# Gated DeltaNet stage of an encoder trunk: TensorE in program order, decays by one-hot products, a new tile order

## The chip, the core and the metric

The kernel runs on one core of a Trainium2 chip. The core has TensorE (PE; PEld is its weight load), VectorE (DVE), ScalarE (ACT), GpSimd (POOL) and SyncE (SP), which here issues every transfer. The metric is the time of one execution in microseconds (us) on the device, of which the median of several runs counts.

## What is computed

The reference is a trunk of two layers with four sub-layers: a mixer of pooling and sparse attention (e), a ConvFFN (f), a Gated DeltaNet mixer (o) and a second ConvFFN (f). Each sub-layer sits in the same frame, and the change concerns the third:

```python
def adaln_post_norm(x, c, mod_w, mod_b, ln_g, ln_b, sublayer):
    mod = jax.nn.silu(c) @ mod_w + mod_b
    shift, scale, gate = jnp.split(mod[:, None, :], 3, axis=-1)
    y = sublayer(x * (1.0 + scale) + shift)
    return layer_norm(DEEPNORM_ALPHA * x + gate * y, ln_g, ln_b)

def gdn_mixer(h, w_in, conv_w, a_log, dt_bias, out_norm, w_out):
    proj = h @ w_in                       # 512 x 1024 times 1024 x 4112
    qkv, gate, beta_raw, a_raw = jnp.split(proj, ODD_SPLITS, axis=-1)
    qkv = jax.nn.silu(causal_dwconv(qkv, conv_w))      # width 4
    ...                                   # 8 heads of 128; q, k normalised
    g = -jnp.exp(a_log) * jax.nn.softplus(a_raw + dt_bias)
    o = gated_delta_rule(l2_norm(q), l2_norm(k), v, beta, g)
    o = rms_norm(o, out_norm) * jax.nn.silu(gate)
    return o @ w_out
```

`gated_delta_rule` needs, for each head and block, decays exp(gc[i] - gc[j]) from the running sum gc of g, the matrix A of products of keys with these decays, the inverse of 1 + A, and then a recurrence over blocks of the sequence with a state of 128x128 for each head.

## The kernel before

**Precision.** A float32 operand is split into a part rounded to fp32r (`hi`) and the rest (`lo`), and a product is made of three passes, hi·hi, hi·lo and lo·hi (`mm3`, L97 to L102). For a weight tile ACT makes `wh` (L93), and DVE or POOL makes `wl` (L94).

**The projection** (`projs`, L144) multiplies the input, held transposed in `h`, with column tiles of 128 weights: 8 slices of the inner dimension, 3 passes, 24 products of 512 columns for each tile. There are 33 tiles: 16 columns for beta and a, then gates g0 to g3, keys k0 to k7, queries q0 to q7, values v0 to v7, gates g4 to g7. The first five are made in two halves of the sequence. Four PSUM buffers (`main`) take the results, three (`chain`) the other work, one (`side`) the modulation.

**Chains.** Each finished tile starts work that follows it: the convolution (`conv_silu`, one ACT pass L949, three DVE passes L951, a Silu L952), then a generator that goes one step further at each `pump` (L66). `k_chain` transposes k (L959), sums squares on ACT, forms A on DVE (L989) and stores it; `q_chain` likewise forms the attention products (L1009 to L1012); `v_chain` stores scaled values. `invert` (L1016) reads the 32x32 diagonal blocks of A back and solves them in 31 steps of two DVE operations (L1029, L1030). `y_chain` (L1040) joins the blocks of two heads into inverses of 128 with small products (L1057 to L1081). `decays` (L937) sends gc through DRAM (`gc_d`) to spread a row over 128 partitions, and makes exp(-|difference|).

**The side work** (`side`, L323) is no part of this sub-layer's data path. It multiplies x with the last norm's gain (`affine`), forms this sub-layer's gate (`mod_gate`, L302) and the shift and scale of the next (`mod_gb`, L286). For each of these three vectors `mod_acc` (L239) loads sixteen 256 KB pieces of a weight into the buffers `mr`, of which there are two; ACT multiplies a piece with c (L255), POOL adds it into `acc` (L257), of which there is one. The gate is spread over the partitions by two pairs of products with ones (L318, L319), whose operands lie in the same two `mr` buffers; shift and scale are summed by transposes (`sum_rows`, L283).

**The recurrence** (`step`, L1134 to L1177) goes over four blocks of 128. Its `state` (L1125) is a tile of the tag `acc`, so that its first write waits until the side work has let go of that buffer. The output projection and the second ConvFFN follow.

**The order.** Each engine executes in its own fixed order. A scheduler with a model of durations puts the instructions of all engines in order when the kernel is built; tile buffers are handed out in program order.

Of the kernel before, what the change touches and what calls it, by code (L numbers as in the profile page):

```python
# [14 lines left out]
P = 128  # L15
S = 512
# [10 lines left out]
class Trunk:  # L27
# [35 lines left out]
    def go(self, gen, rate=1):  # L63
        self.gens.append((gen, rate))
# [13 lines left out]
    BUFS = {"wr": 3, "wh": 5, "wl": 5, "h4": 8, "g4": 14, "t": 4, "c": 5, "sub": 1, "x": 4, "xn": 2, "gate": 1, "mr": 2, "acc": 1}  # L78
# [38 lines left out]
    EARLY = 4  # L117

    def tiles(self, kind):
# [3 lines left out]
        if kind == "o":  # L123
            cols = [(b + n * P, P) for b in (3 * D, D, 0, 2 * D) for n in range(8)]
            return [(4 * D, 16)] + cols[:self.EARLY] + cols[8:] + cols[self.EARLY:8]
# [18 lines left out]
    def projs(self, src, tiles, h, start=None, lo_eng=None):  # L144
# [5 lines left out]
        if start is None:  # L150
            ws = self.pre
            pss = [self.ps("main" if n < 4 else "side") for n in range(first)]
            for half in (slice(0, S // 2), slice(S // 2, S)):
                for n, (t, w, p) in enumerate(zip(tiles, ws, pss)):
                    inst = self.proj(p[:t[1]], w, h, half)
                    if half.start == 0 and n in self.TURN:
                        self.after(self.turns[self.TURN[n]], inst)
# [19 lines left out]
        AHEAD = 2  # L177
        ahead = [self.load_w(src, *t, lo_eng) for t in tiles[first:first + AHEAD]]
        for t, p in zip(tiles, pss):
            yield p[:t[1]]  # L180
        for n in range(first, len(tiles)):
            m = tiles[n][1]
            p = self.ps("main")
            self.proj(p[:m], ahead.pop(0), h)
            if n + AHEAD < len(tiles):
                ahead.append(self.load_w(src, *tiles[n + AHEAD], lo_eng))
            yield p[:m]
# [114 lines left out]
    def mod_gate(self, i):  # L302
# [9 lines left out]
        for h in range(2):  # L312
# [3 lines left out]
            nc.gpsimd.tensor_tensor(lo, part, hi.bitcast(F32), op=ALU.subtract)  # L316
            p = self.ps("side")
# [523 lines left out]
    def odd(self, i, l, h):  # L841
# [38 lines left out]
        gc_d = dram("gc_d", [NB, H, P])  # L880
# [5 lines left out]
        def gate(hd, p):  # L886
            gt = self.b("t", [P, S])
            self.silu = nc.scalar.activation(gt, p, AF.Silu)
            nc.sync.dma_start(og_d[hd], gt)

        def scalars(ba):
# [11 lines left out]
            self.after(inst, self.silu)  # L903
            self.after(nc.scalar.activation(alg, alg, AF.Exp), inst)
# [14 lines left out]
            mm(p[:32, NH:NH + P], g, up, start=True, stop=True)  # L919
            gr = self.b("c", [NH, P])  # L920
            nc.scalar.activation(gr, p[:32, NH:NH + P], AF.Copy)
            nc.sync.dma_start(gc_d.rearrange("t h s -> (t h) s"), gr)
            mm(p[:, :NH], up, g, start=True, stop=True)
            nc.vector.tensor_copy(gc, p[:, :NH])
# [4 lines left out]
            nc.scalar.activation(ex, p[:, :3 * NH], AF.Exp)  # L929
# [16 lines left out]
        def conv_silu(c0, p, out):  # L946
# [5 lines left out]
            inst = nc.scalar.activation(out, t, AF.Silu)  # L952
            self.after(inst, self.exp)
            return inst
# [19 lines left out]
        def k_chain(hd):  # L974
            yield
# [279 lines left out]
```

## Time and profile before

| | us |
|---|---|
| median of 3 runs | 1344.11 (1343.6 to 1347.73) |
| the profiled execution's own time | 1341.34 |
| its span, first to last instruction | 1339.6 |
| PE busy over the span | 1254.1 (94%) |
| DVE / ACT / POOL busy | 832.3 / 602.0 / 404.9 |
| mean granted TensorE clock | 0.971 |

Times within the profile count from the start of the span. A granted clock of 1.00 is the upper of TensorE's two levels (2.4 GHz); 0.50 would be the lower (1.2 GHz), and a stretch in between has had both. An engine's busy time counts each instruction once where they overlap. A row of waits names the engine that waited, the line it then ran, and what ended the wait.

### The profile page before, as it was taken

The numbers are of one execution on the slowest core, as the hardware profiler recorded it, in microseconds if no ns is written. First come the engines' busy times: TensorE is split into PE (matmuls) and PEld (weight loads), VectorE is DVE, ScalarE is ACT, GpSimd is POOL, SyncE is SP. The second block draws the span as 40 slices with busy tenths as digits, with TensorE's granted clock in tenths as the row PEclk, the third lists the DMA queues.
The fourth block names the chain that finished last, engine by engine and source line by source line (L and its number), as shares of the span: only waits on it lengthen the run. The fifth ranks groups of instructions, "written<-read, shape, count | busy, mean of one in ns | idle before, by whom it ended". The sixth has DMA issues, their size and how long they took to land.

```text
span 1339.6 us, 17376 instructions
## 1 busy us (share of the span) xinstructions
PE 1254.1 (94%) x6339; PEld 1023.6 (76%) x6339; DVE 832.3 (62%) x1374; ACT 602.0 (45%) x1107; POOL 404.9 (30%) x324
## 2 busy tenths in 40 slices
PE   4998999999999999999888878989899999999997
PEld 3666656888888888889676666878798888888885
DVE  5599853476877653463767994437647675555328
ACT  3565665653433342345366444545555343334220
POOL 4477666500100000017367675510281010000001
PEclk9999899999999999999988988989999999999998
DMA  9953444146555332513656438674144643323221
GB/s 271 241 166 106 155 149 136 35 127 214 186 180 172 127 110 95 143 48 98 156 165 175 125 102 204 197 261 145 59 127 126 204 128 100 103 79 110 95 63 63
DMA packets 227320, 185.79 MB, mean 139 GB/s; under 512 B 24813, under 2 KB 196058, under 8 KB 227234
## 3 DMA queue, kind: packets, MB, share of 16 engines
q1 hardware_dynamic: 227234, 184.68, 46.2%
q8 instruction: 50, 0.82, 0.3%
q14 instruction: 36, 0.29, 0.1%
HBM read 170.87 MB, written 13.65 MB: 138 GB/s over the span
## 4 chain that ended last, share of the span: by engine, by line
PE 66%; DVE 11%; DMA 10%; POOL 5%; ACT 4%; issue 3%; SPq 1%; DVEq 0%; ACTq 0%; POOLq 0%
PE main L99 16%; PE main L100 16%; PE main L101 16%; DMA mr<-in_f_mod_w_dram 3%; POOL acc L257 3%; PE chain L100 2%; PE chain L101 2%; PE chain L99 2%; DMA wr<-in_e_w_in_dram 2%; DVE t L951 2%; DVE xn L1030 2%; DVE sub L1029 2%; DMA mr<-in_o_mod_w_dram 1%; PE side L99 1%; PE side L100 1%
## 5 line engine op out<-in xcount | busy, mean ns | idle before, releaser
L100 PE MATMUL main<-h,wh 128*128 128x512 f32 (+3 forms) x1104 | 418.0, 380 | 1.7 <-DVE h L409 1.7
L99 PE MATMUL main<-h,wh 128*128 128x512 f32 (+3 forms) x1104 | 414.7, 381 | 2.3 <-ACT h L408 2.1
L101 PE MATMUL main<-h,wl 128*128 128x512 f32 (+3 forms) x1104 | 416.2, 378 | 0.0
L93 ACT ACTIVATE wh<-wr 128x1024 fp32r<-128x1024 f32 x176 | 184.2, 1049 | 292.3 <-PE main L100 196.7
L94 DVE TENSOR_TENSOR wl<-wr,wh 128x1024 fp32r<-128x1024 f32 x126 | 160.9, 1280 | 198.0 <-ACT wh L93 197.8
L99 PEld LDWEIGHTS main<-h,wh 128*128 128x128 f32 (+2 forms) x1104 | 208.9, 191 | 43.4 <-ACT h L408 3.1
L100 PEld LDWEIGHTS main<-h,wh 128*128 128x128 f32 (+2 forms) x1104 | 210.3, 191 | 40.2 <-DVE h L409 2.9
L101 PEld LDWEIGHTS main<-h,wl 128*128 128x128 f32 (+2 forms) x1104 | 210.0, 190 | 37.2 <-issue 0.4
L442 POOL TENSOR_TENSOR rstd<-rstd,mhalf 128x1 f32<-128x1 f32 x16 | 10.4, 650 | 523.2 <-DVE rstd L441 511.7
L94 POOL TENSOR_TENSOR wl<-wr,wh 128x1024 fp32r<-128x1024 f32 (+1 forms) x50 | 119.6, 2396 | 52.1 <-ACT wh L93 45.0
L257 POOL TENSOR_TENSOR acc<-acc,mr 128x512 f32<-128x512 f32 x84 | 109.2, 1306 | 68.4 <-ACT mr L255 60.9
L489 DVE SCALAR_TENSOR_TENSOR t<-main,cw,t 128x511 f32<-128x511 f32 (+1 forms) x164 | 121.5, 744 | 2.1
L255 ACT ACTIVATE mr<-mr,cs 128x512 f32<-128x512 f32 x84 | 60.2, 721 | 80.6 <-DMA mr<-in_f_mod_w_dram 49.8
L951 DVE SCALAR_TENSOR_TENSOR t<-main,ocw,t 128x511 f32<-128x511 f32 (+2 forms) x72 | 53.3, 741 | 32.4 <-ACT t L949 31.5
L487 ACT ACTIVATE t<-main,cb,cw 128x512 f32<-128x512 f32 x82 | 62.3, 761 | 0.0
L310 POOL TENSOR_TENSOR acc<-acc,mr 1x512 f32<-1x512 f32 x8 | 11.8, 1488 | 143.2 <-issue 71.5
L494 ACT ACTIVATE t<-t 128x512 f32<-128x512 f32 x42 | 26.4, 629 | 61.9 <-DVE t L489 61.6
L99 PE MATMUL main<-wh,h 128*128 128x512 f32 x128 | 50.2, 392 | 0.0
L100 PE MATMUL main<-wl,h 128*128 128x512 f32 x128 | 50.0, 391 | 0.0
L101 PE MATMUL main<-wh,h 128*128 128x512 f32 x128 | 49.8, 390 | 0.0
L356 DVE TENSOR_TENSOR h<-chain,h 128x256 fp32r<-128x256 f32 x48 | 19.5, 419 | 35.1 <-ACT h L355 34.7
L352 ACT ACTIVATE chain<-chain,B,G 128x128 f32<-128x128 f32 x84 | 33.1, 438 | 9.9 <-PE chain L344 9.6
(383 smaller groups left out, 2103.4 us busy)
## 6 DMA issues: line engine op xcount, KB each, us to landing
wr<-in_f_w_up_dram SPq DMA_DIRECT2D x84, 512.0 KB
wr<-in_f_w_down_dram SPq DMA_DIRECT2D x42, 512.0 KB
mr<-in_f_mod_w_dram SPq DMA_DIRECT2D x64, 256.0 KB
wr<-in_o_w_in_dram SPq DMA_DIRECT2D x32, 512.0 KB
g<-in_e_mod_w_dram SPq DMA_DIRECT2D x32, 256.0 KB
g<-in_f_mod_w_dram SPq DMA_DIRECT2D x16, 512.0 KB
g<-in_o_mod_w_dram SPq DMA_DIRECT2D x16, 512.0 KB
wr<-in_e_w_in_dram SPq DMA_DIRECT2D x11, 512.0 KB
```

What stands on the lines that cost most here:

```text
L93: nc.scalar.activation(hi, src, AF.Copy)
L94: (lo_eng or nc.vector).tensor_tensor(lo, src, hi.bitcast(F32), op=ALU.subtract)
L99: inst = mm(ps, l[0], r[0], start=start, stop=False)
L100: mm(ps, l[0], r[1], start=False, stop=False)
L101: mm(ps, l[1], r[0], start=False, stop=stop)
L255: inst = nc.scalar.activation(r, raw, AF.Copy, scale=c)
L257: nc.gpsimd.tensor_tensor(part, part, r, op=ALU.add)
L352: nc.scalar.activation(t[:, c, :], t[:, c, :], AF.Identity, scale=G[:, k:k + 1], bias=B[:, k:k + 1])
L487: nc.scalar.activation(t, p, AF.Identity, bias=cb[:, n:n + 1], scale=cw[:, 4 * NF + n:4 * NF + n + 1])
L489: nc.vector.scalar_tensor_tensor(t[:, k:], p[:, :S - k], cw[:, 2 * NF * (2 - k) + n:2 * NF * (2 - k) + n + 1], t[:, k:], op0=ALU.mult, op1 ...
L951: nc.vector.scalar_tensor_tensor(t[:, k:], p[:, :S - k], cw[:, 24 * (3 - k) + n:24 * (3 - k) + n + 1], t[:, k:], op0=ALU.mult, op1=ALU.add)
L1029: nc.vector.tensor_tensor(tv, As[:, j + 1:, j:j + 1].to_broadcast([P, n, m]), Xs[:, j:j + 1, :m].to_broadcast([P, n, m]), op=ALU.mult)
```

## The change

In the region of the projection PE now executes in program order (`manual_schedule`), and the other engines keep the scheduler. The chains are written later: `k_chain` and the others pass one or two pumps more before each product, so that PE meets them about two tiles after their tile. The order of tiles is a table (`ORDER`): g4 ahead of the keys, g5 among the queries. Four weight tiles get their `wl` on DVE instead of POOL (`QUIET`). The decays come from products with one-hot rows, without DRAM. The side work starts at k2 with one step a pump instead of three at q0, rests from q0 to g5, and goes on from q6 with one step a pump; what is left runs in `drain`, after the last tile. `t` has five buffers instead of four, and weights are loaded three tiles ahead instead of two.

```diff
-    BUFS = {..., "t": 4, "c": 5, "sub": 1, ...}
+    BUFS = {..., "t": 5, "c": 5, ...}
...
+    ORDER = [(t[0], int(t[1])) for t in ("g0 g1 g2 g3 g4 k0 k1 k2 k3 k4 k5 k6 k7 q0 q1 q2 q3 g5 "
+                                         "q4 q5 q6 q7 v0 v1 v2 v3 v4 v5 v6 v7 g6 g7").split()]
+    QUIET = [("q", 5), ("q", 6), ("q", 7), ("v", 0)]
+    YS = [("v", 1), ("v", 3), ("v", 5), ("v", 7)]
...
-            for half in (slice(0, S // 2), slice(S // 2, S)):
-                for n, (t, w, p) in enumerate(zip(tiles, ws, pss)):
-                    inst = self.proj(p[:t[1]], w, h, half)
+            for n, (t, w, p) in enumerate(zip(tiles, ws, pss)):
+                inst = self.proj(p[:t[1]], w, h, slice(0, S // 2))
...
-        AHEAD = 2
+        AHEAD = 3 if self.kind == "o" else 2
...
+        for t, w, p in zip(tiles, ws, pss):
+            if start is None:
+                self.proj(p[:t[1]], w, h, slice(S // 2, S))
             yield p[:t[1]]
...
         acc = yield from self.mod_acc(i, j)
+        yield
         o = self.s([P, KC], f"modc{j}")
...
             nc.gpsimd.tensor_tensor(lo, part, hi.bitcast(F32), op=ALU.subtract)
+            yield
             p = self.ps("side")
             nc.tensor.matmul(p, self.ones, hi, start=True, stop=False)
...
-        def decays():
-            for hd in range(H):
-                r = self.b("c", [P, NB, P])
-                nc.sync.dma_start(r, gc_d[:, hd:hd + 1, :].rearrange("t o s -> o t s").partition_broadcast(P))
-                nc.vector.tensor_tensor(r, r, bc(hcol(gc, hd), P), op=ALU.subtract)
-                nc.vector.scalar_tensor_tensor(r, r, -1.0, r, op0=ALU.mult, op1=ALU.min)
-                self.exp = nc.scalar.activation(dec(hd), r, AF.Exp)
+        def decays(heads):
+            for hd in heads:
+                p = self.ps()
+                for n, r in enumerate(self.rows):
+                    mm(p, sel[:, hd, :], r[0], start=n == 0, stop=n == 1)
+                nc.vector.tensor_tensor(v4(p), v4(p), bc(hcol(gc, hd), P), op=ALU.subtract)
+                nc.scalar.activation(p, p, AF.Abs)
+                inst = nc.scalar.activation(dec(hd), v4(p), AF.Exp, scale=-1.0)
...
         def k_chain(hd):
-            yield
+            for _ in range(3 if hd < 2 else 2):
+                yield
...
-            nc.vector.tensor_tensor(hcol(rb, hd), hcol(rk, hd), hcol(beta, hd), op=ALU.mult)
-            nc.vector.tensor_tensor(hcol(br2, hd), hcol(rb, hd), hcol(rk, hd), op=ALU.mult)
+            nc.gpsimd.tensor_tensor(hcol(rb, hd), hcol(rk, hd), hcol(beta, hd), op=ALU.mult)
+            nc.gpsimd.tensor_tensor(hcol(br2, hd), hcol(rb, hd), hcol(rk, hd), op=ALU.mult)
...
-        self.go(self.side(i), 3)
...
+        with self.tc.manual_schedule(engines={mybir.EngineType.PE}):
+            out = self.projs(win, self.tiles("o"), h, self.begin, lo)
...
+            for kind, hd in self.ORDER:
+                p = next(out)
...
+                elif kind == "k":
+                    conv(D + hd * P, p, kh(hd))
+                    if hd < 3:
+                        decays(range(3 * hd, min(H, 3 * hd + 3)))
...
+                    if hd == 2:
+                        side = self.go(self.side(i))
+                    self.go(k_chain(hd))
+                elif kind == "q":
...
+                    if hd in (0, 6):
+                        side[1] = hd // 6
+                    if hd == 2:
+                        self.go(invert())
...
+                if (kind, hd) in self.YS:
+                    self.go(y_chain(self.YS.index((kind, hd))))
+                self.pump()
         self.drain()
```

The order of instructions moves in three places that matter here. In the rows a number at the end of a name is a tile's own; L99 to L101 become L101 to L103, L318 and L319 become L330 and L331, L283 becomes L294, L252 becomes L262. The first place is PE where the gate's products (`side<-mr,ones`) stand. Before, the first pair is behind tile q5, and the second pair within q6 and q7:

```order
L100 MATMUL main_6372<-h_819_4162,wh_6200 128x512
L101 MATMUL main_6372<-h_815_4158,wl_6201 128x512
L318 MATMUL side_6428<-mr_6424,ones 128x512
L319 MATMUL side_6428<-mr_6425,ones 128x512
L99 MATMUL main_6494<-h_812_4155,wh_6300 128x512
```

Now both pairs stand behind g7, the last tile (`main_7287`):

```order
L102 MATMUL main_7287<-h_819_4162,wh_7066 128x512
L103 MATMUL main_7287<-h_815_4158,wl_7067 128x512
L330 MATMUL side_7315<-mr_7242,ones 128x512
L331 MATMUL side_7315<-mr_7243,ones 128x512
L1117 MATMUL chain_7323<-c_7265,c_7264 64x64 x8
L991 MATMUL chain_7333<-ident,t_7150 128x128 x4
L1100 MATMUL chain_7341<-c_7285,xn_6702 32x32 x16
L330 MATMUL side_7361<-mr_7319,ones 128x512
L1108 MATMUL chain_7372<-ident,g_1285_7201 64x64 x8
L331 MATMUL side_7361<-mr_7320,ones 128x512
```

The pairs moved by nine and more tiles to the end. The second place is SP, where the next sub-layer's shift and scale are loaded (`mr<-in_f_mod_w`). Before, the first of the 32 loads stands among the weights of the queries and values:

```order
L107 DMA wr_6931<-in_o_w_in_dram 128x8x128
L252 DMA mr_6441<-in_f_mod_w_dram 128x512
L884 DMA at_d<-c_6489 128x4x128
L252 DMA mr_6444<-in_f_mod_w_dram 128x512
L252 DMA mr_6447<-in_f_mod_w_dram 128x512
L107 DMA wr_7023<-in_o_w_in_dram 128x8x128
```

Now the first stands behind the last value that is stored, and the recurrence's loads (L1180) stand among them:

```order
L902 DMA og_d<-t_7312 128x512
L115 DMA wr_8029<-in_o_w_out_dram 128x1024
L895 DMA vb_d<-c_7338 128x4x128
L262 DMA mr_7366<-in_f_mod_w_dram 128x512
L1180 DMA xn_7564<-og_d 128x8x128
L262 DMA mr_7369<-in_f_mod_w_dram 128x512
L1180 DMA xn_7572<-og_d 128x8x128
L1180 DMA h_1359_7558<-vb_d 128x1024
L1180 DMA h_1360_7560<-kd_d 128x1024
```

All 32 loads moved behind the projection. The third place is PE between the first and the second block of the recurrence. Before, the last sums of the shift (`side<-ident,acc`) stand within the last tile, ahead of the recurrence's first product:

```order
L101 MATMUL main_7512<-h_814_4157,wl_7427 128x512
L1064 MATMUL chain_7443<-c_7397,xn_6812 32x32 x5
L283 MATMUL side_6958<-ident,acc_6715 128x128 x4
L1064 MATMUL chain_7443<-c_7397,xn_6812 32x32 x11
L99 MATMUL main_7512<-h_815_4158,wh_7426 128x512
```

Now all four sets stand behind the first block (L1207 to L1248), ahead of the second (L1195):

```order
L1222 MATMUL main_7606<-c_7586,h_1361_7562 128x128 x4
L1248 MATMUL chain_7682<-ident,h_1359_7558 128x128 x4
L1248 MATMUL chain_7690<-ident,h_1359_7558 128x128 x4
L294 MATMUL side_7461<-ident,acc_7365 128x128 x4
L294 MATMUL side_7467<-ident,acc_7365 128x128 x4
L294 MATMUL side_7538<-ident,acc_7474 128x128 x4
L294 MATMUL side_7544<-ident,acc_7474 128x128 x4
L1195 MATMUL main_7620<-acc_7557,g_974_5086 128x128 x2
```

The four sets moved from within the projection to between two blocks of the recurrence.

## Rows read from the trace of the kernel before

**Rows 1.** The page, part 1: busy time by engine.
```profile
PE 1254.1 (94%) x6339; PEld 1023.6 (76%) x6339; DVE 832.3 (62%) x1374; ACT 602.0 (45%) x1107; POOL 404.9 (30%) x324
```
**Rows 2.** Stretches: length, busy us of PE, PEld, DVE, ACT, POOL, clock, DMA share, GB/s.
```profile
626.50:892.00 265.50, 228.52 (x1244) 186.62 (x1244) 177.95 (x290) 128.47 (x289) 154.60 (x102) 0.92 0.62 173
735.00:805.00 70.00, 55.56 (x263) 45.56 (x261) 68.51 (x102) 29.15 (x86) 49.31 (x34) 0.93 0.45 118
880.00:900.00 20.00, 16.76 (x141) 13.88 (x141) 6.61 (x10) 8.14 (x14) 3.00 (x3) 0.83 0.82 303
```
**Rows 3.** Waits of PE from 626 to 892: total us, times, longest.
```profile
PE chain L959 <- ACT g L952: 13.0, 5, 4.3
...
PE side L283 <- POOL acc L257: 2.1, 2, 1.9
```
**Rows 4.** Timeline of PE: start, us; two products of a whole tile that follow each other.
```profile
650.12 0.39 PE L99 MATMUL main<-h,wh 128*128 128x512 f32 x1
650.35 0.39 PE L100 MATMUL main<-h,wh 128*128 128x512 f32 x1
```
**Rows 5.** Chain that ended last, 800 to 905: start, us to the next piece, what.
```profile
838.99 1.76 PE chain L1057 x16
...
845.04 1.02 PE chain L1064 x32
846.06 0.59 PE chain L959 x4
...
894.00 1.08 PE chain L1074 x16
...
895.75 1.14 PE chain L1081 x16
...
902.96 0.89 PE main L1152 x8
```
**Rows 6.** Timeline of DVE (then one row of POOL) around the inverse.
```profile
729.58 1.13 DVE L989 SCALAR_TENSOR_TENSOR g<-chain,br,g 128x128 f32<-128x128 f32 x4
...
741.18 0.20 DVE L1029 TENSOR_TENSOR sub<-xn,xn 128x31 f32<-128x31 f32 x1
...
754.03 2.44 DVE L1029 TENSOR_TENSOR sub<-xn,xn 128x192 f32<-128x192 f32 x1
...
757.87 0.37 DVE L1029 TENSOR_TENSOR sub<-xn,xn 128x207 f32<-128x207 f32 x1
...
803.93 1.03 DVE L1033 COPY xn<-xn 128x1024 f32<-128x1024 f32 x1
...
753.76 2.49 POOL L94 TENSOR_TENSOR wl<-wr,wh 128x1024 fp32r<-128x1024 f32 x1
```
**Rows 7.** Groups of DVE from 700 to 892: busy us, mean ns, idle before.
```profile
L1030 DVE TENSOR_TENSOR xn<-xn,sub 128x31 f32<-128x31 f32 (+15 forms) x31 | 23.3, 750 | 0.7
L1029 DVE TENSOR_TENSOR sub<-xn,xn 128x31 f32<-128x31 f32 (+15 forms) x31 | 22.6, 729 | 0.6
```
**Rows 8.** Line L1057, its products on PE: shortest, median, longest ns, first and last start.
```profile
L1057 PE MATMUL chain<-g,g x64: 217/275/294, 816.4 to 877.6; 128*128 128x64 f32 x64
```
**Rows 9.** Chain that ended last, 800 to 905, where it runs through the side work.
```profile
863.27 0.73 ACT mr L255
864.07 1.29 POOL acc L257
865.38 2.90 DMA mr<-in_f_mod_w_dram
868.37 0.73 ACT mr L255
869.17 1.30 POOL acc L257
870.49 2.83 DMA mr<-in_f_mod_w_dram
...
875.53 4.16 DMA mr<-in_f_mod_w_dram
```
**Rows 10.** Timelines of POOL and PE: last sum of the side work, first product of block 1.
```profile
883.97 1.27 POOL L257 TENSOR_TENSOR acc<-acc,mr 128x512 f32<-128x512 f32 x1 [2.14 <-ACT mr L255]
...
901.90 1.06 PE L1146 MATMUL main<-acc,g 128*128 128x128 f32 x8
```
**Rows 11.** Groups of POOL from 626 to 892: busy us, mean ns, idle before.
```profile
L316 POOL TENSOR_TENSOR mr<-acc,mr 128x512 fp32r<-128x512 f32 x2 | 2.8, 1387 | 0.0
```

More of the change, by code (lines that the diff above doesn't have):

```diff
@@ L63, in go @@
     def go(self, gen, rate=1):
-        self.gens.append((gen, rate))
+        item = [gen, rate]
+        self.gens.append(item)
+        return item
     def pump(self, n=1):
@@ L76, in drain @@
             self.pump()
-    BUFS = {"wr": 3, "wh": 5, "wl": 5, "h4": 8, "g4": 14, "t": 4, "c": 5, "sub": 1, "x": 4, "xn": 2, "gate": 1, "mr": 2, "acc": 1}
+    BUFS = {"wr": 3, "wh": 5, "wl": 5, "h4": 8, "g4": 14, "t": 5, "c": 5, "x": 4, "xn": 2, "gate": 1, "mr": 2, "acc": 1}
     def b(self, tag, shape, dt=F32):
@@ L176, in projs @@
                     next(start)
-        AHEAD = 2
-        ahead = [self.load_w(src, *t, lo_eng) for t in tiles[first:first + AHEAD]]
-        for t, p in zip(tiles, pss):
+        AHEAD = 3 if self.kind == "o" else 2
+        eng = lambda n: lo_eng[n] if isinstance(lo_eng, list) else lo_eng
+        ahead = [self.load_w(src, *t, eng(first + n)) for n, t in enumerate(tiles[first:first + AHEAD])]
+        for t, w, p in zip(tiles, ws, pss):
+            if start is None:
+                self.proj(p[:t[1]], w, h, slice(S // 2, S))
             yield p[:t[1]]
@@ L185, in projs @@
             if n + AHEAD < len(tiles):
-                ahead.append(self.load_w(src, *tiles[n + AHEAD], lo_eng))
+                ahead.append(self.load_w(src, *tiles[n + AHEAD], eng(n + AHEAD)))
             yield p[:m]
@@ L916, in scalars @@
             nc.vector.scalar_tensor_tensor(th(g), th(t3), -1.0, over(alg, NB), op0=ALU.mult, op1=ALU.mult)
+            yield
             p = self.ps()
[L919 to L924, printed above, removed]
+            for tb in range(NB):
+                mm(pc(p, tb)[:H], g[:, tb * H:(tb + 1) * H], up, start=True, stop=True)
+            for t in self.rows:
+                t.append(self.b("c", [H, S], F32R))
+            rh, rl = (t[0] for t in self.rows)
+            nc.scalar.activation(rh, p[:H], AF.Copy)
+            nc.vector.tensor_tensor(rl, p[:H], rh.bitcast(F32), op=ALU.subtract)
             p = self.ps()
@@ L951, in conv_silu, with silu @@
                 nc.vector.scalar_tensor_tensor(t[:, k:], p[:, :S - k], cw[:, 24 * (3 - k) + n:24 * (3 - k) + n + 1], t[:, k:], op0=ALU.mult, op1=ALU.add)
-            inst = nc.scalar.activation(out, t, AF.Silu)
-            self.after(inst, self.exp)
-            return inst
+            late.append(lambda: nc.scalar.activation(t if out is None else out, t, AF.Silu))
+            return t
+        def silu():
+            for fn in late:
+                inst = fn()
+                self.after(inst, self.exp)
+                if self.hold is None:
+                    self.hold = inst
+            late.clear()
         def tok_major(src):
@@ L1082, in y_chain @@
             nc.scalar.activation(y[:64, :, 64:], w64(p), AF.Copy)
-        YS = (1, 3, 5, 7)
-        out = self.projs(win, self.tiles("o"), h, self.begin, nc.gpsimd)
-        ba = self.b("c", [16, S])
-        nc.scalar.activation(ba, next(out), AF.Copy)
-        for hd in range(self.EARLY):
-            gate(hd, next(out))
-        scalars(ba)
-        decays()
-        for hd in range(H):
-            inst = conv_silu(D + hd * P, next(out), kh(hd))
-            if hd == 0:
-                self.hold = inst
-            self.go(k_chain(hd))
-            self.pump()
@@ L1117, in odd @@
-        for hd in range(self.EARLY, H):
-            gate(hd, next(out))
-            if hd + 5 in YS:
-                self.go(y_chain(YS.index(hd + 5)))
-            self.pump()
+        silus, late, self.exp, self.rows = [], [], None, ([], [])
+        sel = self.b("xn", [H, H, P], F32R)
+        nc.vector.tensor_copy(sel, self.ident[:H, :H].unsqueeze(2).to_broadcast([H, H, P]))
+        lo = [nc.gpsimd] * (len(self.ORDER) + 1)
+        for kind, n in self.QUIET:
+            lo[1 + self.ORDER.index((kind, n))] = nc.vector
```

83 lines of the change are left out of this document (51 added, 32 removed).

## The prediction

> **What bounds the kernel now.** I read four views: busy times, stretches, PE's waits, and the chain that ended last.
>
> PE is busy for 94% of the span [rows 1], so the end moves with what PE does and with where it stands still. The first five tiles of this stage end at 626.5 us and its last tile at about 892, and in these 265.5 us PE is busy for 228.5 at a mean clock of 0.92 [rows 2]. That is where the change can win. The waits there are single gaps of up to 4.3 us, most of them a key's or query's transposition that waits for the Silu [rows 3].
>
> A second bound hides beneath PE. From 816 to 881 the chain that ended last runs mostly through the side work: load a piece into `mr`, scale it on ACT, add it on POOL, and only then is its buffer free for the next load [rows 9]. The last of these sums ends at 885.2, the first product that reads the recurrence's state starts at 901.9 [rows 10], and PE waits for this work for 2.1 us in all [rows 3]. It is just in time now because it runs while PE still projects. The recurrence's state needs the `acc` buffer, so block 1 cannot start before the last of the three modulation vectors is summed.
>
> **The change, part by part.** I reckon two points: T, the end of the last tile (892 now), and S, the start of block 1 (901.9 now). Behind S the program is the same, so the time moves as S does.
>
> *PE's own work up to T.* At the upper clock a product of 512 columns follows the last after 0.228 us [rows 4]. 28 whole tiles of 24 come to 153.2. Sixteen key and query heads take four transposes (0.59) and eight product rows (0.89) each [rows 5], 23.7 together; eight values 4.7. A pair of heads in the joining of inverses costs 1.76 + 1.02 + 1.08 + 1.14, and about 0.54 for eight transposes at the rate of L1074 [rows 5], so four pairs 22.2. New are 16 one-hot products at 0.228, 3.7, and small ones for 1. Sum 208.5. By the order, 4.4 of it stands behind the last tile. T can't be earlier than 626.5 + 204.1 = 830.6.
>
> *The wait for the inverse.* PE can no longer go round a late operand, and the largest is the solved diagonal blocks that L1093 (L1057 before) reads behind tile v2. By the order, the last key's A stands behind tile q2: 626.5 + 12 tiles (65.6) + decays and small products (4.7) + eight transpositions (4.7) and eight sets of product rows (7.1) = 708.6. From A on DVE to the first step of the solution took 11.6, from 729.58 to 741.18 [rows 6], mostly A's way through memory, so 720.2. I add 5, because POOL and the DMA queue have two pieces of side work there for each tile. The solution then took 62.8, to 803.93 [rows 6], of which 45.9 were its own 62 operations [rows 7]; DVE was busy for 68.5 of those 70 us [rows 2]. From the copy at its end to L1057 passed another 12.5 [rows 6, 8].
>
> How long the 62 operations take depends on POOL. Of two nearly equal steps one took 2.44 us and one 0.37, and the long one lies on a POOL subtraction of 2.49 us [rows 6]. So I count 22 us for the operations alone and 8 for the short POOL operations that stay among them, as the order puts the weight subtractions of this stretch on DVE; with five tiles' convolutions, attention products and two subtractions (16) that is 46 instead of 62.8. The Trainium skill, SBUF — State Buffer, section Who interferes with whom, states that a VectorE instruction with two SBUF inputs is fully blocked by a GpSimd instruction that reads SBUF; the trace agrees, as the two rows show. By that rule alone, with POOL silent, the stretch would be 38 and T 8 us earlier; without it, at the old pace, T would be 17 later.
>
> So L1093 runs at 708.6 + 11.6 + 5 + 46 + 12.5 = 783.7. Behind it stand seven tiles (38.3), the joining but for its end (17.8) and five values (3.0), 59.1 in all: **T = 843**, between 831 (no wait) and 866 (inverse at its old pace and 6 more). Against 892 that is a gain of 49.
>
> *The side work behind T.* This is the price. The gate's two pairs of products now stand behind the last tile, and they read the two `mr` buffers. Until they have run, none of the 32 loads for the next shift and scale can start; before, they started among the queries and values. The second pair needs a copy on ACT and a subtraction on POOL of 1.39 us [rows 11] after the first: 5 us behind T, at 848. Then each buffer goes round through load (2.8 to 2.9 us, with a 4.2), ACT (0.73) and POOL (1.30), once in 5.1 us: from 865.38 to 870.49 and on to 875.53 [rows 9]. Two buffers make that 2.55 us a load, 81.6 for 32; the first two of each sixteen need no sum, which saves 2.6. The extremes are 2.43 (load, ACT and POOL with no gap) and 3.1 (with the load of 4.16). Among the first ten loads stand fifteen of 512 KB for the recurrence: 10.5 MB, 34.6 us at the highest rate of a stretch, 303 GB/s [rows 2], instead of 25.5, so 9 more (3 to 15). The turn between the two sums and the transposes and the state's copy at the end take 7. **S = 848 + 79 + 9 + 7 = 943**, 41 us later than now. Meanwhile PE has only block 0 of the recurrence.
>
> *Parts that cost nothing.* The decays lose their eight transfers through memory, which helps the keys begin earlier; that is in T, since no wait for Silus is left in it. Two ACT passes a head instead of one (8 × 0.6 us) lie on ACT, which is busy for 128 of 265.5 [rows 2]. The key factors on POOL and the third weight tile ahead lie beside PE; if POOL becomes the limit there, the 5 us above are too few. The other sub-layers get the same extra steps in their side work and nearly the same order; I count them as 0, within 2 either way.
>
> *Sum.* The profiled execution took 1341.3 and gains 41: 1382.3. It lies 2.8 under the median of the runs, so I forecast **1385**.
>
> **Rivals.** *The side work keeps up: faster.* If loads ran ahead and only POOL's 1.3 us counted, 32 pieces would take 41 us, and with T at 831 block 1 would start at 831 + 5 + 41 + 7 = 884, 18 earlier: 1326. It decides at 1.5 us a load for T = 843, or 1.8 for T = 831. For it speaks that all other traffic has then gone; against it that the load is the longest part of each round even at the end of the stage [rows 9], and two buffers can't hide it. The Trainium skill, Perfetto Trace Analysis, section Identifying the Most-Contended Engine, says to improve the engine with the highest occupancy first, which here is PE, and by that rule the filled gaps would come out as time saved; the trace agrees only up to T. Chance 0.08.
>
> *PE starves: much slower.* In program order each late operand stops all tiles behind it. If POOL (weights, sums and key factors in one queue) or the transfers fall behind, T comes at 866 or later, and with a slow round of the loads S lies at 975 to 995: 1417 to 1437. For it speaks how full DVE is around the inverse [rows 2]; against it that the chains stand two tiles behind and weights three tiles ahead. Chance 0.17.
>
> *The two cancel: no change.* With T = 831 and 1.8 us a load the time stays within 4 us. It needs both at once: 0.03.
>
> **How the numbers follow.** The forecast's own case, S later by 16 (T 831, 2.43 a load, 3 for the recurrence's loads) to 70, has 0.72, that is 1360 to 1414. A measurement of this kernel tells 0.3%, 4 us, from no change. Faster takes 0.08, the same 0.03, slower 0.72 + 0.17 = 0.89. The range leaves out the faster rival and the upper part of the starved case, and goes somewhat below the forecast's own lower end for an inverse and loads that both do better: 1352 to 1418.
>
> **What would show it.** Right: the last tile at 831 to 866; the gate's products directly behind it; 32 loads of `mr` behind them at about 2.5 us each; a gap of 70 to 90 us on PE before L1195, with the clock at its lower level in it, ended by POOL's sum and the transposes; block 1 at about 943, and from there on the old lengths. The inverse should lose its operations of over 2 us. Wrong: loads of that work between the tiles, a round of the buffers under 3.6 us, or block 1 before 902. If T lies beyond 870, the starved case holds.

## The result, and the profile after

The change takes 1407.56 us (median of 4 runs, 1402.83 to 1414.99) against 1345.92 for the kernel before in the same comparison: a ratio of 1.046, with a 95% interval of 1.040 to 1.052. The forecast was 1385 in a range of 1352 to 1418: the direction and the range hold, and the forecast is 23 us too low. The profiled execution took 1406.3, its span is 1404.6.

Page, part 1, busy time by engine; PE has the busy time of [rows 1] in a span 65 us longer:

```profile
PE 1254.5 (89%) x6359; PEld 1026.3 (73%) x6359; DVE 804.9 (57%) x1356; ACT 614.1 (44%) x1117; POOL 396.6 (28%) x336
```

Stretches of the changed kernel, columns as in [rows 2]; the first answers to its second row:

```profile
735.00:805.00 70.00, 56.63 (x273) 47.52 (x272) 55.57 (x103) 25.77 (x72) 34.91 (x22) 0.90 0.46 117
805.00:862.00 57.00, 57.00 (x438) 47.64 (x437) 23.03 (x33) 19.53 (x30) 8.85 (x7) 1.00 0.41 113
862.00:902.00 40.00, 16.73 (x156) 14.40 (x154) 11.54 (x15) 15.55 (x36) 9.20 (x7) 0.69 0.75 261
902.00:945.00 43.00, 2.23 (x8) 1.43 (x8) 2.06 (x6) 12.98 (x18) 19.31 (x16) 0.50 0.40 123
```

Around the inverse PE stands for 13.4 us, from 805 to 862 not at all; in the 83 us that follow it works for 19. What it waits for, 626 to 1000, answers to [rows 3]:

```profile
PE side L294 <- POOL acc L267: 63.1, 3, 34.6
PE chain L991 <- DVE c L1047: 8.9, 2, 6.2
PE chain L1248 <- DVE h L1241: 8.5, 1, 8.5
PE main L1207 <- DMA h<-vb_d: 6.9, 1, 6.9
PE chain L991 <- ACT g L976: 4.4, 1, 4.4
```

The wait for POOL's sum, 2.1 us before, is 63.1. Where the last tile ends, on PE's timeline:

```profile
862.40 0.40 PE L103 MATMUL main<-h,wl 128*128 128x512 f32 x1
862.63 0.39 PE L330 MATMUL side<-mr,ones 128*128 128x512 f32 x1
862.86 0.40 PE L331 MATMUL side<-mr,ones 128*128 128x512 f32 x1
...
865.87 0.50 PE L330 MATMUL side<-mr,ones 128*128 128x512 f32 x1
866.52 0.63 PE L1108 MATMUL chain<-ident,g 64*64 64x64 f32 x8
867.09 0.49 PE L331 MATMUL side<-mr,ones 128*128 128x512 f32 x1
```

The gate's products stand directly behind the last tile; the first load into a freed `mr` is issued at 866.4. The chain that ended last (start, us to the next piece) does not go through these loads at first. It runs through the last value's way through memory and block 0, and comes to a load of the side work only behind a load of the recurrence on SP's queue (SPq, L1180), which had waited for block 0:

```profile
865.67 5.69 DMA vb_d<-c
...
871.43 6.08 DMA h<-vb_d
...
877.55 3.48 PE main L1207 x16
...
898.20 0.37 SPq L1180
...
898.67 4.42 DMA mr<-in_f_mod_w_dram
```

From there it goes round like this until block 1 starts:

```profile
931.54 2.62 DMA mr<-in_f_mod_w_dram
934.24 0.73 ACT mr L265
935.03 1.27 POOL acc L267
936.32 2.62 DMA mr<-in_f_mod_w_dram
...
959.05 1.27 POOL acc L267
960.37 1.13 PE side L294 x4
...
964.82 2.08 PE main L1195 x8
```

A buffer's round is 4.78 us there (931.54 to 936.32), so 2.4 us a load with two buffers; 5.1 and 2.55 were reckoned from [rows 9]. The first product of block 1 is at 964.8, where it was at 901.9 [rows 10].

Three points hold the account. P is the 2100th product of the three-pass kind in the records, late in the sub-layer before this one (the expectations call it a triple product; a few records are missing, so it is good to about 1 us). T is the end of the last tile, S the first product of block 1.

| | P | T - P | S - T | end - S |
|---|---|---|---|---|
| before | 592.9 | 299.2 | 9.8 | 437.7 |
| change | 601.5 | 261.3 | 102.0 | 439.8 |
| difference | +8.6 | -37.9 | +92.2 | +2.1 |

The four sum to the 65.0 us by which the span grew. The stretch from P to T became 38 us shorter, and the tail behind it costs 92.

### The profile page after: what moved, and what is told of

It is laid out like the page before. It is cut to its first block, busy times and chain, and to the rows that moved or that the text cites. A ratio compares the mean times of both kernels' runs of the same rounds, so it can differ in the third digit from the quotient of the medians.

```text
span 1404.6 us, 17405 instructions
## 1 busy us (share of the span) xinstructions
PE 1254.5 (89%) x6359; PEld 1026.3 (73%) x6359; DVE 804.9 (57%) x1356; ACT 614.1 (44%) x1117; POOL 396.6 (28%) x336
## 4 chain that ended last, share of the span: by engine, by line
PE 69%; DVE 9%; DMA 8%; POOL 6%; ACT 4%; issue 2%; SPq 1%; DVEq 0%; ACTq 0%; POOLq 0%
PE main L101 17%; PE main L102 17%; PE main L103 17%; DMA mr<-in_f_mod_w_dram 3%; POOL acc L267 2%; PE chain L102 2%; PE chain L103 2%; PE chain L101 2%; POOL wl L96 2%; ACT mr L265 1%; PE side L101 1%; PE side L102 1%; PE side L103 1%; DVE xn L1066 1%; DMA mr<-in_o_mod_w_dram 1%
## 5 line engine op out<-in xcount | busy, mean ns | idle before, releaser
L101 PE MATMUL main<-h,wh 128*128 128x512 f32 (+2 forms) x1104 | 414.8, 380 | 2.4 <-ACT h L420 2.1
L102 PE MATMUL main<-h,wh 128*128 128x512 f32 (+2 forms) x1104 | 413.4, 375 | 1.9 <-DVE h L368 1.1
L103 PE MATMUL main<-h,wl 128*128 128x512 f32 (+2 forms) x1104 | 413.1, 375 | 0.0
L96 DVE TENSOR_TENSOR wl<-wr,wh 128x1024 fp32r<-128x1024 f32 x130 | 166.1, 1280 | 202.2 <-ACT wh L95 202.2
L101 PEld LDWEIGHTS main<-h,wh 128*128 128x128 f32 (+1 forms) x1104 | 207.9, 189 | 43.8 <-ACT h L420 2.7
L102 PEld LDWEIGHTS main<-h,wh 128*128 128x128 f32 (+1 forms) x1104 | 208.1, 189 | 40.3 <-DVE h L368 2.0
L103 PEld LDWEIGHTS main<-h,wl 128*128 128x128 f32 (+1 forms) x1104 | 208.2, 189 | 37.5 <-issue 0.4
L96 POOL TENSOR_TENSOR wl<-wr,wh 128x1024 fp32r<-128x1024 f32 (+1 forms) x46 | 109.7, 2388 | 59.8 <-ACT wh L95 46.6
L294 PE MATMUL side<-ident,acc 128*128 128x128 f32 x48 | 9.3, 326 | 64.3 <-POOL acc L267 63.1
L294 PEld LDWEIGHTS side<-ident,acc 128*128 128x128 f32 x48 | 6.7, 165 | 67.2 <-POOL acc L267 65.5
L506 ACT ACTIVATE t<-t 128x512 f32<-128x512 f32 x42 | 26.4, 629 | 59.1 <-DVE t L501 58.9
L101 PE MATMUL main<-wh,h 128*128 128x512 f32 x128 | 50.2, 392 | 0.0
L103 PE MATMUL main<-wh,h 128*128 128x512 f32 x128 | 49.8, 390 | 0.0
```

What stands on the lines that cost most here:

```text
L96: (lo_eng or nc.vector).tensor_tensor(lo, src, hi.bitcast(F32), op=ALU.subtract)
L101: inst = mm(ps, l[0], r[0], start=start, stop=False)
L102: mm(ps, l[0], r[1], start=False, stop=False)
L103: mm(ps, l[1], r[0], start=False, stop=stop)
L294: self.nc.tensor.transpose(p[:, k * P:(k + 1) * P], acc[:, k * P:(k + 1) * P], self.ident)
L506: nc.scalar.activation(av[0], av[0], AF.Silu)
```

## The experiments

Each ratio is to the kernel before, run on the same chip beside it. All the runs that have a time are in one table, P, T and S from one profile of each. e3, the changed kernel with four buffers `mr`, has none: its buffers need 200 KB a partition, and 196.75 KB are there.

| run | P | T | S | median us | ratio, 95% |
|---|---|---|---|---|---|
| e1, side work early | 598.4 | 880.7 | 901.1 | 1346.02 | 1.001 (0.999 to 1.003) |
| e2, before with it late | 599.4 | 871.3 | 972.5 | 1417.11 | 1.054 (1.050 to 1.058) |
| e4, steps only here | 596.3 | 856.2 | 959.5 | 1404.72 | 1.045 (1.040 to 1.050) |
| e5, three `mr` | 600.7 | 866.3 | 948.1 | 1388.52 | 1.032 (1.030 to 1.035) |
| e6, rest in the inverse | 600.5 | 896.8 | 916.9 | 1357.54 | 1.009 (1.007 to 1.012) |
| e7, and other subtractions | 602.4 | 896.8 | 918.0 | 1356.26 | 1.008 (1.005 to 1.010) |
| e8, before again | 595.1 | 894.8 | 904.6 | 1343.95 | one run |
| e9, free order on PE | 602.5 | 858.0 | 961.0 | 1401.82 | 1.041 (1.036 to 1.047) |
| e10, combined, three `mr` | 602.4 | 887.7 | 899.8 | 1337.12 | 0.994 (0.992 to 0.996) |
| e11, combined, two `mr` | 606.5 | 878.7 | 892.4 | 1335.59 | 0.990 (0.986 to 0.994) |
| e12, e11 with free order | 604.5 | 855.8 | 891.4 | 1331.74 | 0.987 (0.983 to 0.990) |
| e13, change again | 601.9 | 863.6 | 967.5 | 1409.73 | one run |

**e1: the side work early.** In the change the side work rests from q0 to q5, g5 among them; here it goes on.

```diff
-                        side = self.go(self.side(i))
+                        side = self.go(self.side(i), 2)
...
-                    if hd in (0, 6):
-                        side[1] = hd // 6
+                    if hd == 2:
+                        side[1] = 1
...
+                    side[1] = 2
                     v = conv(2 * D + hd * P, p)
```

> The changed kernel, with one thing undone: the side work goes at two steps a tile, one from q2 to q7, two again from v0, and never rests. So the gate's two pairs of products stand behind q3 and g5 on PE instead of behind the last tile, and the sums of scale and shift stand behind v2 and behind v7 and g6. Theory (the loss is the tail: from T = 862 to S = 965 PE waits for loads that could not start before the gate's products): loads start near 740, the last sum ends by 850, T stays at 862 to 880, block 1 starts 8 to 12 us behind T, at 872 to 890 instead of 965, and the time is 1313 to 1333, some 80 us under the change and 12 to 30 under the kernel before. Rival A (program order on PE is the loss, wherever the side work stands): the waits move between the tiles, T goes beyond 900 and the time stays over 1370. Rival B (POOL's sums now fall into the inverse and hold DVE): T 885 to 900, time about 1344, no gain over before.

Measured 1346.02. The tail is gone: S - T falls from 102 to 20, and S lies 64 us earlier than in the change. That is the theory's main claim, and it stands. But there is no gain over before, so the sum of the theory was wrong: T came at 881, and S 20 us behind it instead of 8 to 12. From its first step to the copy at its end the inverse took 55.5 us, where the change's took 46.7. PE's waits from 640 to 930:

```profile
PE chain L991 <- DVE c L1047: 10.5, 1, 10.5
PE chain L991 <- ACT g L976: 6.0, 1, 6.0
PE main L1208 <- DMA h<-vb_d: 4.1, 1, 4.1
PE side L294 <- DVE modc L295: 3.1, 1, 3.1
PE chain L1093 <- POOL acc L267: 2.9, 1, 2.9
PE side L331 <- POOL mr L327: 2.4, 1, 2.4
```

Rival A falls. Rival B's time fits, and its T nearly (881, where it had 885 to 900), but not all of its place: some waits lie around the inverse (the first two), others are PE's own turn at products and sums of the side work. How the 21 us by which T - P is longer than in the change divide between the two isn't shown. Behind T stand the joining's end (881 to 889), the wait for the last value's way through memory (4.1) and block 0 (893 to 901).

**e2: the kernel before, with the tail put in.** The scheduler, decays and tile order are those of before; the side work has the pace of the change, and its gate products are held behind the last tile's:

```diff
             p = self.ps("side")
-            nc.tensor.matmul(p, self.ones, hi, start=True, stop=False)
+            inst = nc.tensor.matmul(p, self.ones, hi, start=True, stop=False)
+            if self.kind == "o":
+                self.after(inst, self.last)
```

> The kernel before, scheduler, decays and tile order as they were, with one thing put in: the gate's products are held behind the last product of the last tile, as in the change, by the same slow and resting rate of the side work and an order on PE. Theory (the price is the tail): T stays at 885 to 892, the 32 loads start behind it and take 94 us as in the changed kernel, block 1 starts at 985 to 995 instead of 902, and the time is 1420 to 1440. Rival (manual order on PE, decays or tile order cost the time, not the place of the side work): the loads keep up behind T at POOL's pace of 1.3 us each, block 1 at 935 to 945, time 1375 to 1390, or no change at all at 1344.

Measured 1417.11, 3 us below the theory's 1420 to 1440 and far from either of the rival's times. The theory had T at 885 to 892 and block 1 at 985 to 995; they came at 871 and 972. PE's waits from 640 to 1000 begin with

```profile
PE side L286 <- POOL acc L260: 69.2, 3, 34.8
```

and S - T is 101.2, as in the change. So the place of two pairs of products, with the pace that puts them there, makes the whole loss without any of the other edits. The run shows a second thing that nobody had asked: T - P fell from 299.2 to 271.9. With the side work out of the way the old order gains 27 of the 38 us that the change gains. For the order of PE, the decays, the tile order and the other edits 10.6 are left. The stretch from P to T in the kernel before, in e2 and in the change, columns as in [rows 2]:

```profile
592.90:892.10 299.20, 262.22 (x1518) 218.58 (x1517) 189.83 (x319) 147.03 (x330) 176.11 (x112) 0.93 0.57 159
599.40:871.30 271.90, 244.89 (x1433) 205.16 (x1432) 175.69 (x307) 125.03 (x293) 139.30 (x83) 0.96 0.50 135
601.50:862.80 261.30, 245.17 (x1465) 206.71 (x1464) 155.44 (x287) 132.86 (x304) 133.57 (x95) 0.97 0.48 131
```

PE stands still for 37.0, 27.0 and 16.1 us of them. So 10 of e2's 27 us are shorter waits, and 17 are less busy time: fewer instructions stand ahead of T, and the granted clock is 0.96 instead of 0.93. The 10.6 that the other edits add are, in sum, waits alone. Which of those edits brings them isn't shown.

**e5: three buffers `mr`.**

```diff
-    BUFS = {"wr": 3, "wh": 5, "wl": 5, "h4": 8, "g4": 14, "t": 5, "c": 5, "x": 4, "xn": 2, "gate": 1, "mr": 2, "acc": 1}
+    BUFS = {"wr": 3, "wh": 5, "wl": 5, "h4": 8, "g4": 14, "t": 4, "c": 5, "x": 4, "xn": 2, "gate": 1, "mr": 3, "acc": 1}
```

> The changed kernel with three buffers mr instead of two, the place for it taken from t (four instead of five, as before the change). Theory (behind T two buffers going round through load, ACT and POOL in 4.84 us set 2.42 us a load): three make it 1.6 us, and POOL's 1.3 is not reached; the 24 loads of the second half take some 40 us instead of 57, the first ten gain less among the recurrence's loads, block 1 starts 17 to 28 us earlier, 937 to 948, and the time is 1380 to 1391. Rival (the transfers or the order on SP's queue set the pace): less than 6 us change, 1401 to 1412. Fewer t may hold up a tile here and there, 0 to 5 us, in T and not behind it.

Measured 1388.52, and S - T is 81.8 instead of 102.0: the theory's time, and a difference of its size. T - P is 265.6 instead of 261.3, within the 0 to 5 us allowed for the missing `t`. POOL's timeline in that run (start, us):

```profile
927.34 1.26 POOL L267 TENSOR_TENSOR acc<-acc,mr 128x512 f32<-128x512 f32 x1 [0.54 <-ACT mr L265]
929.28 1.26 POOL L267 TENSOR_TENSOR acc<-acc,mr 128x512 f32<-128x512 f32 x1 [0.68 <-ACT mr L265]
931.01 1.26 POOL L267 TENSOR_TENSOR acc<-acc,mr 128x512 f32<-128x512 f32 x1 [0.47 <-ACT mr L265]
```

A sum every 1.7 to 1.9 us instead of 2.4: the number of buffers sets the pace once the recurrence's loads are through, and the rival, under 6 us of change, falls. The theory's place for the gain holds only in half. From T to the issue of the seventeenth load passed 48.8 us instead of 58.8, and from there to S 33.0 instead of 43.2, so 10 of the 20 us came in the first sixteen loads, though the theory expected less gain among the recurrence's loads.

**e6 and e7: the side work around the inverse.** In e6 it takes two steps a tile up to q1, none until q6, then two from q7, so that its additions miss the inverse, and the sums of shift are held behind the last tile (those lines are left out below); e7 is e6 and moves the subtractions that DVE takes over:

```diff
...
+                if side is not None:
+                    side[1] = {"q2": 0, "q7": 2, "v4": 3, "v5": 2, "g6": 1}.get(f"{kind}{hd}", side[1])
...
-    QUIET = [("q", 5), ("q", 6), ("q", 7), ("v", 0)]
+    QUIET = [("v", 0), ("v", 1), ("v", 2), ("v", 3), ("v", 4)]
```

> The changed kernel with the side work laid around the inverse: two steps a tile from k2 to q1, none from q2 to q6, two from q7 (gate's products behind q7 and v0), both sums of scale behind v4, and the sums of shift held behind the last tile. In the run with the side work early POOL's 1.3 us additions fell into the inverse, DVE had ten steps of over 1 us there, and T was 881 instead of 862. Theory (the additions in the inverse cost those 18 us): the inverse is as in the changed kernel (737 to 786), T 860 to 868, loads from 790 to 872, block 1 at 880 to 892, time 1321 to 1334. Rival (T at 881 came from waits of PE for the side work's own products, which stand between the tiles again): T 875 to 885 and block 1 at 895 to 905, time 1338 to 1350.

> The kernel of the run before in this list, and the weight subtractions that DVE takes over from POOL are those of v0 to v4 instead of q5, q6, q7 and v0, since in the changed kernel those of v1 to v4 ran on POOL inside the inverse (747, 755, 765, 773), each beside a step of 2.4 us. Theory (a POOL operation holds a DVE step for its length): four steps of 2.4 us fall to 0.4, four subtractions of 1.2 come, the inverse ends 3 to 5 us earlier and the time falls by as much. Rival (DVE is the full engine there, 19.3 of 20 us, whoever holds it): no change within 2 us.

e6 missed: 1357.54, slower than both guesses. The inverse is as the theory had it (736.4 to 786.2), but T is 896.8, for a reason of its own. First row of PE's waits from 640 to 960 in e6:

```profile
PE side L296 <- POOL acc L269: 20.0, 1, 20.0
```

Behind the second pair of products, at 787.6, the sixteen loads of the scale took until 837.6, 3.1 us each beside the weights instead of the 2.5 that I had reckoned, and PE stood in front of the sums with five tiles behind them. So e6 can't tell its theory from its rival, and whether the additions in the inverse cost T 18 us stays open.

e7 can be read, since the inverse lies ahead of that wait. Two steps of it in the change, on DVE's timeline:

```profile
746.27 1.38 DVE L1065 TENSOR_TENSOR c<-xn,xn 128x231 f32<-128x231 f32 x1
747.68 2.45 DVE L1066 TENSOR_TENSOR xn<-xn,c 128x231 f32<-128x231 f32 x1
```

The weight subtraction on POOL's timeline that lies on the second:

```profile
747.34 2.53 POOL L96 TENSOR_TENSOR wl<-wr,wh 128x1024 fp32r<-128x1024 f32 x1
```

And the same two steps in e7 on DVE's timeline, with the subtraction now behind them there:

```profile
746.84 1.38 DVE L1069 TENSOR_TENSOR c<-xn,xn 128x231 f32<-128x231 f32 x1
748.25 0.40 DVE L1070 TENSOR_TENSOR xn<-xn,c 128x231 f32<-128x231 f32 x1
...
749.46 1.22 DVE L97 TENSOR_TENSOR wl<-wr,wh 128x1024 fp32r<-128x1024 f32 x1
```

The step of 2.45 is one of 0.40; all four steps over 2 us are gone, and the inverse's own operations take 26.3 us, where e6's took 33.5. Yet from its first step to the end of its copy it takes 48.5 instead of 49.8, and it ends 1.1 us earlier, not 3 to 5. DVE spends most of what the steps no longer lose on the work that it took over: weight subtractions take 6.1 us of that stretch instead of 1.2, and the copy takes 2.2 instead of 1.1. The rival's forecast holds, no change within 2 us, but the time is no test of the inverse here, as the 20 us wait lies behind it in both runs. The Trainium skill, SBUF — State Buffer, section Who interferes with whom, states that a VectorE instruction with two SBUF inputs contends with a GpSimd instruction that reads SBUF, and that the ports they share are an exclusive lock; the rows agree for the single step. The stretch shows that handing the blocking work to DVE gives back only the difference.

**e4, e8, e13: why P is late.** e4 keeps the two added steps of the side work in this sub-layer only:

```diff
         acc = yield from self.mod_acc(i, j)
-        yield
+        if self.kind == "o":
+            yield
...
-            yield
+            if self.kind == "o":
+                yield
```

> The changed kernel, with the two added steps of the side work (one behind the sums of a vector, one ahead of the gate's products) taken out of the other sub-layers and kept in this one. In the profile of the changed kernel this stage starts 8.7 us later than before, a loss that was there by 222 us, in the first sub-layer. Theory (the added steps shift the order there): the 8.7 us come back, the time is 1397 to 1401. Rival (the buffers that changed, t with five and the c in place of sub, or the placement of the program as a whole, make it): the stage starts as late as in the change, time within 4 us of 1407.

> The kernel before, unchanged, for a second profile: when does its last sub-layer but one reach the same product of its projection (the 2100th triple product of the program, at 592.9 in the first profile, 601.5 in the changed kernel)? Theory (the added steps of the side work delay the first sub-layer by 8.7 us): 591 to 595 again. Rival (the first sub-layer varies from run to run by as much): anything from 590 to 602.

> The changed kernel, unchanged, for a second profile. The 2100th triple product of the program stood at 592.9 and 595.1 in two profiles of before, at 601.5 in the first of the change; the runs without the added steps have it at 596.3, 602.4 and 606.5. Theory (the added steps are not the cause, the first sub-layer ends earlier or later by itself): anywhere from 593 to 607. Rival (the change delays it): 600 to 603 again. T minus that point was 261.3 and S minus T 102.0: both should come again within 5.

e4 alone looked like the theory (P 596.3), but its interval can't be told from the change's. e10, e11 and e12 lack the added steps too and have P at 602.4, 606.5 and 604.5, so the steps are not the cause. Before came at 592.9 and 595.1, the change at 601.5 and 601.9, the others from 596.3 to 606.5. e2 has the first sub-layer of before with one added step, and 599.4. What delays P by some 7 us in the change stays open. In e13 T - P is 261.7 and S - T 103.8: these repeat.

**e9: the order on PE left to the scheduler.**

```diff
-        with self.tc.manual_schedule(engines={mybir.EngineType.PE}):
+        if True:
```

> The changed kernel with the order of PE left to the scheduler again, as before the change; the chains two tiles behind, the one-hot decays, the tile order and the pace of the side work stay. Built so, the gate's products still stand behind the last tile. Theory (the loss is the place of the side work's products and not the program order of PE): the tail of some 102 us stays, T within 10 us of 862, time 1396 to 1420. Rival (program order on PE stops tiles behind late operands, and that is what the change pays for): T 10 to 25 us earlier, time 1380 to 1395.

Measured 1401.82, with an interval that overlaps the change's, and a tail of 102.9. Program order on PE isn't the loss, and it is no gain that the intervals can tell either: T - P is 255.5 with the scheduler's order and 261.3 without.

**e10 to e12: what the runs pointed to.** e11 starts the side work early as in e1, with the sums of scale a tile later, the last value's chain a tile earlier, the added steps in this sub-layer only, and e7's subtractions; e10 has three `mr` as well, and e12 is e11 with the edit of e9:

```diff
+                    side[1] = {"q2": 1, "v1": 2, "v2": 1, "v3": 2, "v4": 3, "v6": 2}.get(f"{kind}{hd}", side[1])
...
         def v_chain(hd, v):
             yield
-            yield
+            if hd < 7:
+                yield
```

> The changed kernel with what the other runs showed: the side work early as in the run with products behind q3 and g5, but both sums of scale one tile later (v3); three mr and four t; the added steps of the side work in this sub-layer only; the weight subtractions of v0 to v4 on DVE; the last value's chain one tile earlier. Theory: the stage starts 4 us earlier (added steps), the waits for the sums of scale (6) and behind POOL (5) shrink with a third buffer, the wait for the last value's transfer (4) goes: against 1346 that is 12 to 18 less, 1328 to 1336. Rival (a third buffer brings POOL's additions into the inverse in denser order and DVE stays the full engine there): T no earlier than 878, time 1340 to 1348.

> The same with two mr and five t, as in the changed kernel. Theory (the third buffer is worth something among the tiles as it is behind them): 4 to 10 us over the run with three. Rival (among the tiles the queue of SP and POOL set the pace): within 3 us of it.

> The combined kernel with two mr, its order on PE left to the scheduler. Theory (program order on PE brings nothing by itself: with the side work behind the last tile the free order had T 5 us earlier, counted from the start of the stage): 1328 to 1337, within 4 us of the combined kernel or faster. Rival (with the side work among the tiles the scheduler puts the products and sums where its own model has them ready, too early for the chip, and PE waits for each): 8 us or more slower, over 1342.

All three beat both kernels, the one before by 0.6 to 1.3% with intervals clear of 1: 1337.12, 1335.59 and 1331.74. S - T is 12.1 and 13.7 in e10 and e11, and PE's wait for the last value's transfer (4.1 in e1) is no longer among its waits in e11. In e10 T is 887.7, as its rival had it, and the time lies just over the theory's 1328 to 1336. The third buffer is worth nothing that can be told among the tiles: two buffers were to cost 4 to 10 us more, and they don't, so the rival of e11 holds. e12 has the time that its theory forecast, and against e11 it is no difference that the intervals can tell; its scheduler brings all tiles to 855.8 and leaves 31 us of PE's work behind them, which ends at the same S within 1 us. Why T - P is 272.2 in e11 and not 261.3, PE's waits from 640 to 900 in it tell:

```profile
PE chain L1048 <- DVE xn L1069: 4.7, 1, 4.7
PE side L332 <- ACT mr L327: 4.3, 1, 4.3
PE side L333 <- POOL mr L328: 4.1, 1, 4.1
PE chain L1096 <- POOL acc L267: 3.4, 1, 3.4
```

Three of the four are the price of the side work among the tiles. In all PE stands still for 22.6 us of the 272.2, where it did for 16.1 in the change; the other 4.4 are longer busy time, with the side work's products back ahead of T.

## Why the prediction was right, and where it was 23 us short

**The tail was right as a mechanism and nearly as a sum.** The gate's products stand directly behind the last tile, and S - T is 102.0 against 100. From T to the first load passed 3.6 us (5 in the sum), from there until the eleventh is issued 40.8 (25.5 + 9), until 960.3, with the last load landed, 53.1 (53.5 for 22 loads), and 4.5 behind that (7). So the term for the recurrence's loads was too small: among them ten loads took 15 us more than the round alone, the upper bound of the 3 to 15 reckoned. Part of that is order: loads of the side work at 895.5 and 898.7 stood in SP's queue right behind loads of the recurrence that waited for block 0. The round at the end is 2.4 us a load (2.55 in the sum). That the sum came out within 2 us owes something to errors that cancel. e1, e2 and e5 show the cause from three sides: take the place away and the tail goes, put it into the kernel before and it comes, add a buffer and it shrinks by a fifth.

**The step that failed is T**, predicted at 843 and found at 862.8, inside 831 to 866. By its own terms:

| term | predicted | measured |
|---|---|---|
| end of the first five tiles | 626.5, as before | 637.4 |
| from there to the last key's A on DVE | 82.1 (708.6) | 87.5 (724.9) |
| A to the first step of the solution | 16.6 | 12.0 |
| the solution, up to its copy | 46 | 46.7 |
| its copy to L1093 | 12.5 | 19.3 |
| L1093 to T | 59.1 | 59.9 |

Eleven of the 20 us are a late start. The prediction counted the rest of the program as 0, within 2 either way, and 6 to 9 were lost ahead of P, by which of two profiles of each kernel are compared. Another 5.4 lie among the keys. Of the 5 us added to A's way through memory 0.4 came.

Inside the inverse the sum had the right size. It shrank from 62.8 to 46.7 us (46 predicted), though the operations of over 2 us, which were to go, stayed in four of its steps: the subtractions of v1 to v4 still ran on POOL there. But the wait for its result, on which the prediction built T, didn't occur: PE came to L1093 after 24 us of unbroken work from 779.3. PE had stopped earlier, for 13.4 us within 735 to 805, on transposes of the chains (L991: 8.9 for DVE's L1047, 4.4 for a Silu), and L1047 stood in one DVE queue with the inverse's steps. The operand that stopped PE in program order was not the largest one, but a small one behind it in the same queue. The sum had put waits for Silus at none.

So the account of T runs along PE and not along the inverse. Its stretch from the first five tiles to T:

```profile
637.40:862.80 225.40, 210.35 (x1187) 174.44 (x1187) 137.50 (x246) 109.81 (x258) 109.70 (x84) 0.97 0.52 140
```

The prediction's T is its bound of 830.6 and 12.4 of waiting at L1093. The measured T is that bound, 10.9 of late start, 15.0 of waiting elsewhere, and 6.3 by which PE was busy longer than the 204.1 reckoned at the upper clock; the granted clock was 0.97. That the waiting came out near 12.4 is luck, as it was another wait.

**Behind S** nothing was counted, and 2.1 us came: at its restart PE takes 2.08 us for eight products (chain above, 964.82), where eight of the recurrence's took 0.89 [rows 5], and its granted clock from 902 to 945 was 0.50.

**The rivals.** "The side work keeps up" is out: 2.4 us a load, where it needed 1.5. "PE starves" needed T at 866 or later and a slow round; T was 3 us short of it and the round wasn't slow, so the time of 1407 came from the forecast's own case, in its upper part (1360 to 1414). One sum there is off: with T at 831, 2.43 us a load and 3 for the recurrence's loads the prediction's own terms put S at 921, 19 later and not 16. The measured time lies far from that end.

**What the prediction did not see** is how little of T's gain belonged to the change's other edits. It took the 49 us at T as the change's own gain. By e2, 27 of the 38 that came are what the tail's work costs when it runs among the tiles of the old order: most of the gain and the price were the same work, moved. e1 shows the converse: with that work back, T - P is 282.3, and the total is that of before.

## What to carry to other kernels

Work that is hidden under a busy engine has a place, a length and a last moment at which it must start. Before crediting a reorder with shorter stretches, follow each buffer of that work to the instruction that frees it: here two pairs of small products held two buffers, and 94 us of loads and sums stood behind them. Try the moved piece alone in the old kernel (e2): it tells at once what the rest of the change is worth. And when one engine's instructions are held up by another's work, moving that work to the held engine gains only the difference: in e7 the steps lost 7.2 us, and 4.9 of subtractions came.

## What was not expected of the hardware

Kernels that hardly differ ahead of P reach it between 592.9 and 606.5. The six runs of e11 fall in two groups, 1326.7 and 1327.7, and 1335.5 to 1336.2, some 8 us apart, with mean granted clocks of 0.974 and 0.977 against 0.969 and 0.970 for the spans. So differences of under 10 us between single profiles of this kernel say little, the late start in the account above among them, although it came twice.
